# Recurrent-chunk keys transposed undecayed, the decay multiplied into the state's update

## The chip, the cores and the metric

One core of one Trainium2 chip runs the whole program. The metric is the device time of one execution in microseconds; the median of several runs is quoted, and lower is better. In the profile PE is TensorE (matmul), PEld its weight loads, DVE is VectorE, ACT is ScalarE, POOL is GpSimd and SP is SyncE, which issues the DMAs.

## The reference, cut to what matters

Two layers of a hybrid block are computed for 256 context and 256 latent tokens of width 2048: a modulated input projection, three groups of heads (retention, latent attention, RWKV-7) with gates, an output projection and a layer norm. The change lies in the RWKV-7 group, which scans the tokens in both directions:

```python
def step(state, inp):
    r_t, w_t, k_t, v_t, a_t, b_t = inp
    sa = jnp.einsum('dbhvk,dbhk->dbhv', state, a_t)
    state = state * w_t[..., None, :] + sa[..., :, None] * b_t[..., None, :] + v_t[..., :, None] * k_t[..., None, :]
    return state, jnp.einsum('dbhvk,dbhk->dbhv', state, r_t)
```

There are 8 heads of 64 channels. The kernel does this scan in chunks of 64 tokens, as matrix products.

## The kernel before, in words

**The work.** In each layer the 8 RWKV heads are done in two halves of 4 heads, and each half in two segments of 256 tokens (context, then latent): 4 segments a layer, 8 in all. A segment has 4 chunks, and both directions `d` are done side by side. The 4 heads of a half lie as 2 tiles `j` of 128 partitions, each with 2 heads `p` of 64 channels (partitions 0 to 63 and 64 to 127).

**A segment, in order.** `prepare` (L702 to L758) makes for each `(d, j)` the scaled queries `AR`, the scaled keys `bf` (channels on the partitions; b and k of each chunk side by side) and `pC`, the product of a chunk's decays for each channel. `grams` (L762) multiplies keys and queries (TensorE, L768), masks the result into `G` (VectorE, L772), and multiplies the keys by `pC` into `bs` (GpSimd, L776). `token_major` (L780) transposes `bs` on TensorE (L783) into a PSUM tile `bkT`, which ScalarE copies to `BK` (L784). `inverse_blocks` (L787) inverts 32x32 triangular blocks: transposes of `G` (L795), then a chain of 31 substitution steps on VectorE (L814, L817) in a tile `S` that GpSimd first fills (L801, L803), then transposes back (L822). `inverse_rest` (L826) completes the inverse with small matmuls `pA` and `pB` (L841), which need `TA` (L833).

**The scan** (L851) takes the 4 chunks in turn. For each: matmuls with the state (L905), with the inverse (L913), with the keys (L923, into the upper half of the PSUM tile `uz[d]`); then VectorE makes the new state `Zb` from that product and from `Zc` (L928 for the first chunk, L930 later), and GpSimd multiplies the new state by the next chunk's `pC` into `Zc` (`decayed`, L889). Then `values` (L866) transposes the next chunk's values on TensorE into the lower columns of the same PSUM tile `uz[d]` (L872, L874), VectorE copies them to `W` (L877), and `from_values` (L880) multiplies them (L884). Where the segment's outputs are wanted, the matmuls L937 stand between L923 and `values`; the context segments of the last layer have none. The last segment of a half needs no state after its last chunk: 28 updates of both directions in all, 24 of them followed by `values` in the same scan. During the scan, hooks call `prepare` for the next segment.

**Order.** TensorE's order is written by hand: `M(what)` lets a number of microseconds (table `FILL`, one set for each layer) of projection and adaptive-norm matmuls (L475, L431) run at that place, as filler under the latencies of the other engines. The order on VectorE, ScalarE and GpSimd is a scheduler's, which goes by priorities (`chain()` raises them) and by a simulated time; it also places the tiles, where tiles of one tag share slots. Tag `bs` has one slot, which `bs`, `S` and `Zc` take in turn. Tag `tb` has six, for `th`, `bf`, `Mt`, `TA` and others. Four PSUM slots (`sm`) hold `gram`, `bkT`, `uz`, `xy` and others.

Of the kernel before, what the change touches and what calls it, by code (L numbers as in the profile page):

```python
# [10 lines left out]
F32 = mybir.dt.float32  # L11
# [3 lines left out]
ALU = mybir.AluOpType  # L15
# [124 lines left out]
def hybrid_kernel(ctx, tc, I, out, dbg=None, layers=L):  # L140
    nc = tc.nc
    dma = nc.sync.dma_start
    act = nc.scalar.activation
    TT = nc.vector.tensor_tensor
    TS = nc.vector.tensor_scalar
    STT = nc.vector.scalar_tensor_tensor
    mm = nc.tensor.matmul

    def copy_a(o, i):
        act(out=o, in_=i, func=AF.Copy)  # L150
# [12 lines left out]
    def pbank(shape, name="sm"):  # L163
        return psm.tile(shape, F32, tag="sm", name=name)
# [5 lines left out]
    def K(name, n=128):  # L170
        o, e = CST[name]
        return cst[:n, o:e]

    idn = K("idn")
# [13 lines left out]
    with tc.tile_pool(name="ini", bufs=1) as ip:  # L188
# [9 lines left out]
        for l in range(layers):  # L198
            p, d = prT[l], dpr[l]
# [149 lines left out]
    def M(what):  # L349
        credit[0] += FILL[now[0]][what] if isinstance(what, str) else what  # L350
        while credit[0] > 0:
            t = next(mainline)
            if t == 0.0:
                settle(credit[0])
                credit[0] = 0.0
                return
            credit[0] -= t
            settle(t)
# [297 lines left out]
    def rwkv(rp, l, last):  # L656
        twl, al = state["lora", l]
        hs = lambda h: slice(64 * h, 64 * h + 64)
# [103 lines left out]
        def grams(S, d, j):  # L762
            ar, bf, mk, NY = S.AR[d], S.bf[d, j], masks[:, d], S.NY
            gps = [pbank([128, 4, 128], "gram") for p in range(2)]
            for i in range(4):
                for p in range(2):
                    hsl = slice(64 * p, 64 * p + 64)
                    mm(gps[p][:, i, :NY], lhsT=bf[hsl, i].rearrange("p a t -> p (a t)"),  # L768
                       rhs=ar[hsl, j, i, :NY], start=True, stop=True)
            for p in range(2):  # L770
                with chain():
                    TT(out=S.G[:, d, :, 2 * j + p, :NY], in0=gps[p][:, :, :NY],  # L772
                       in1=mk[:, :NY].unsqueeze(1).to_broadcast([128, 4, NY]), op=ALU.mult)

            bs = rp.tile([128, 4, 128], F32, tag="bs", name="bs", bufs=1)
            nc.gpsimd.tensor_tensor(out=bs, in0=bf.rearrange("p c a t -> p c (a t)"),  # L776
                                    in1=S.pC[d][:, j].unsqueeze(2).to_broadcast([128, 4, 128]), op=ALU.mult)
            return bs

        def token_major(S, d, j, bs):  # L780
            tp = pbank([128, 4, 128], "bkT")
            for i in range(4):
                nc.tensor.transpose(tp[:, i], bs[:, i], idn)  # L783
            act(out=S.BK[d][:, :, j, :], in_=tp, func=AF.Copy)  # L784

        def inverse_blocks(S):
# [66 lines left out]
        def scan(S, hook):  # L853

            rF, kF, vF = S.F
            s0, need, AR, BK, pC = S.s0, S.need, S.AR, S.BK, S.pC
            G = [S.G[:, d] for d in range(2)]
            Y = S.Y = rp.tile([128, 4, 256], F32, tag="Y", name="Y", bufs=1)
            Zc = rp.tile([128, 2, 2, 128], F32, tag="bs", name="Zc", bufs=1)
# [27 lines left out]
            def decayed(d, i):  # L887
                with chain():
                    nc.gpsimd.tensor_tensor(out=Zc[:, d], in0=Z[d],  # L889
                                            in1=pC[d][:, :, i:i + 1].to_broadcast([128, 2, 128]), op=ALU.mult)  # L890
# [9 lines left out]
            for i in range(4):  # L900
                for d in range(2):
                    if Z[d] is not None:
                        for j in range(2):
                            for r in halves:
                                mm(xy[d][r, 128 * j:128 * j + 128], lhsT=AR[d][:, j, i, r], rhs=Z[d][:, j, :],  # L905
                                   start=False, stop=(d == 1 and j == 1 and r.start == 0))
                with chain():
                    copy_a(Y[0:64, i % 2::2, :], xyt[0:64])
                hook(f"A{i}")
                M("xy")  # L910
                for d in range(2):
                    for h in range(4):
                        mm(uz[d][0:64, hs(h)], lhsT=G[d][0:64, i, h, 0:64], rhs=Y[0:64, 2 * d + i % 2, hs(h)],  # L913
                           start=True, stop=True)
                    with chain():
                        copy_a(W[d][0:64], uz[d][0:64, 0:256])
                M("u")
                if not (S.seg == 1 and i == 3):
                    for d in range(2):
                        zp = uz[d][:, 256:384].rearrange("p (j e) -> p j e", j=2)  # L920
                        for h in range(4):
                            j, p = divmod(h, 2)
                            mm(zp[hs(p), j], lhsT=BK[d][:, i, j, hs(p)], rhs=W[d][:, hs(h)], start=True, stop=True)  # L923
                        Zn = Zb[d][i % 2]
                        with chain():
                            for p in range(2):
                                if Z[d] is None:
                                    nc.vector.tensor_copy(out=Zn[hs(p), :, hs(p)], in_=zp[hs(p)])  # L928
                                else:
                                    TT(out=Zn[hs(p), :, hs(p)], in0=Zc[hs(p), d, :, hs(p)], in1=zp[hs(p)], op=ALU.add)  # L930
                        Z[d] = Zn
                        if i < 3:
                            decayed(d, i + 1)
                if need:
                    for d in range(2):
                        for h in range(4):
                            mm(xy[d][64:128, hs(h)], lhsT=G[d][0:64, i, h, 64:128], rhs=W[d][0:64, hs(h)], start=False,  # L937
                               stop=(d == 1 and h == 3))
                    for d in range(2):
                        c = 3 - i if d else i  # L940
                        if i < 2:
                            copy_a(Y[64:128, c], xy[d][64:128])
                        else:
                            TT(out=Y[64:128, c], in0=Y[64:128, c], in1=xy[d][64:128], op=ALU.add)
                if i < 3:
                    hook(f"B{i}")
                    M("zq")
                    for d in range(2):
                        values(d, i + 1)
                    M("zp")  # L950
                    for d in range(2):
                        from_values(d, i + 1)
# [47 lines left out]
        S, before = Segment(0), None  # L1000
# [3 lines left out]
        for n in range(4):  # L1004
# [8 lines left out]
            S.BK = [rp.tile([128, 4, 2, 128], F32, tag="BK", name="BK", bufs=2) for d in range(2)]  # L1013
            copies = []
            for d, j in ORDER:
                bs = grams(S, d, j)
                copies.append(lambda d=d, j=j, bs=bs: token_major(S, d, j, bs))
                M("gram")
                if len(copies) > 1:
                    copies.pop(0)()  # L1020
                M("tp")
# [23 lines left out]
            S = N  # L1045
# [589 lines left out]
```

## Time and profile before

| | |
|---|---|
| median of 3 runs | 2083.82 us (2076.26 to 2086.75) |
| the profiled execution's own time | 2067.83 us |
| its span, first to last instruction | 2066.1 us |
| PE busy | 1936.9 us, 94% |
| DVE busy | 1177.7 us, 57% |
| ACT busy | 768.8 us, 37% |
| POOL busy | 677.7 us, 33% |
| mean granted TensorE clock | 0.975 of full speed |

The RWKV segments lie at about 240 to 640 us (layer 0) and 1316 to 1730 us (layer 1) of the span. Busy time says little by itself: where PE is the busiest engine, what counts is where it stands idle, for how long, and at which clock it runs.

### The profile page before, as it was taken

To read this page: it belongs to the slowest core of one execution; us is meant where nothing else is said; L and a number is where in the kernel's file an instruction comes from. 1 tells how busy PE (TensorE), PEld (TensorE's weight loads), DVE (VectorE), ACT (ScalarE), POOL (GpSimd) and SP (SyncE) were. 2 spreads that over 40 slices of the span, in tenths; PEclk is the share of its full clock that TensorE was granted. 3 is DMA by queue.
4 is the path that set the end of the run, shared out by engine and by line. 5 is a ranking of instruction groups with operands and counts; after the bars stand their busy time and mean duration, and the time that the engine had idled before them with its cause. 6 is when DMAs were issued, how large, how long until landed. Compare 5 with 4: busy or idle time off the path is not lost. (4 is left out here: it accounts for less than half of the span.)

```text
span 2066.1 us, 35249 instructions
## 1 busy us (share of the span) xinstructions
PE 1936.9 (94%) x13222; PEld 1507.0 (73%) x13222; DVE 1177.7 (57%) x2905; ACT 768.8 (37%) x1443; POOL 677.7 (33%) x640
## 2 busy tenths in 40 slices
PE   6999999999999999999999989999799999899896
PEld 3567767676677687877788778776467678799875
DVE  3446576857662444445643582475648572564857
ACT  2223333333422444444222243332333334665542
POOL 0000444554534311223000175643335446323402
PEclk9999999999999999999999999997999999999998
DMA  9984453425255644449463343320822133534864
GB/s 327 368 266 118 120 157 107 151 80 169 62 169 188 197 147 138 134 131 334 136 194 128 108 138 107 89 83 18 310 82 78 41 107 113 171 108 130 268 230 163
DMA packets 255468, 318.42 MB, mean 154 GB/s; under 512 B 28288, under 2 KB 171968, under 8 KB 254400
## 3 DMA queue, kind: packets, MB, share of 16 engines
q1 hardware_dynamic: 255296, 316.16, 48.2%
q8 instruction: 104, 1.70, 0.3%
q14 instruction: 68, 0.56, 0.1%
HBM read 290.64 MB, written 25.46 MB: 153 GB/s over the span
## 5 line engine op out<-in xcount | busy, mean ns | idle before, releaser
L475 PE MATMUL pm<-H,whi 128*128 128x512 f32 (+2 forms) x2880 | 849.1, 375 | 12.8 <-DVE stg L634 4.1
L254 POOL TENSOR_TENSOR wlo<-raw,whi 128x512 fp32r<-128x512 f32 x332 | 438.9, 1329 | 989.5 <-ACT whi L253 885.8
L475 PEld LDWEIGHTS pm<-H,whi 128*128 128x128 f32 (+1 forms) x2880 | 513.9, 191 | 156.1 <-issue 55.6
L253 ACT ACTIVATE whi<-raw 128x512 fp32r<-128x512 f32 x556 | 348.9, 630 | 701.6 <-PE pm L475 356.7
L475 PE MATMUL pm<-H,wlo 128*128 128x512 f32 (+2 forms) x1440 | 536.1, 372 | 8.7 <-POOL wlo L254 8.7
L475 PEld LDWEIGHTS pm<-H,wlo 128*128 128x128 f32 (+1 forms) x1440 | 276.0, 192 | 62.0 <-issue 10.7
L254 DVE TENSOR_TENSOR wlo<-raw,whi 128x512 fp32r<-128x512 f32 x224 | 155.7, 700 | 187.0 <-ACT whi L253 172.7
L1411 PE MATMUL acc<-whi,Y 128*128 128x512 f32 x768 | 240.8, 393 | 0.5 <-ACT whi L253 0.5
L1411 PEld LDWEIGHTS acc<-whi,Y 128*128 128x128 f32 x768 | 143.5, 188 | 30.7 <-ACT whi L253 0.9
L1411 PE MATMUL acc<-wlo,Y 128*128 128x512 f32 x384 | 150.6, 392 | 0.2 <-DVE wlo L254 0.2
L814 DVE TENSOR_TENSOR stmp<-S,Mt 128x60 f32<-128x60 f32 (+14 forms) x488 | 110.9, 267 | 10.7 <-POOL S L803 10.6
L817 DVE TENSOR_TENSOR S<-S,stmp 128x60 f32<-128x60 f32 (+14 forms) x488 | 107.8, 261 | 0.4
L475 PE MATMUL pmx<-H,whi 128*128 128x512 f32 (+1 forms) x256 | 82.9, 402 | 14.7 <-ACT H L375 7.5
L431 PE MATMUL adap<-raw,scv 128*32 128x512 f32 x512 | 70.1, 620 | 15.1 <-DMA raw<-in_w_ada 11.8
L1411 PEld LDWEIGHTS acc<-wlo,Y 128*128 128x128 f32 x384 | 72.1, 188 | 15.8 <-DVE wlo L254 1.0
L150 ACT ACTIVATE Y<-xy 64x512 f32<-64x512 f32 (+1 forms) x56 | 26.7, 498 | 131.5 <-PE xy L905 99.3
L475 PEld LDWEIGHTS pmx<-H,whi 128*128 128x128 f32 x256 | 50.0, 206 | 31.6 <-DVE H L376 9.1
L751 DVE SCALAR_TENSOR_TENSOR bf<-th,kkF 128x256 f32<-128x256 f32 x32 | 16.3, 509 | 73.5 <-ACT th L726 73.2
L930 DVE TENSOR_TENSOR Zb<-Zc,uz 64x128 f32<-64x128 f32 x96 | 27.4, 285 | 52.7 <-PE uz L923 42.7
L889 POOL TENSOR_TENSOR Zc<-Zb,pC 128x256 f32<-128x256 f32 x56 | 33.9, 616 | 59.8 <-DVE Zb L930 31.0
L772 DVE TENSOR_TENSOR G<-gram,masks 128x512 f32<-128x512 f32 (+1 forms) x64 | 37.1, 620 | 23.5 <-PE gram L768 23.1
L475 PE MATMUL pmx<-H,wlo 128*128 128x512 f32 (+1 forms) x128 | 49.6, 388 | 0.0
(301 smaller groups left out, 2875.1 us busy)
## 6 DMA issues: line engine op xcount, KB each, us to landing
raw<-in_w_in SPq DMA_DIRECT2D x388, 256.0 KB, 3.0
raw<-in_w_ada SPq DMA_DIRECT2D x64, 1024.0 KB, 5.5
xraw<-in_w_ada SPq DMA_DIRECT2D x32, 1024.0 KB, 8.0
raw<-in_w_out SPq DMA_DIRECT2D x128, 256.0 KB, 3.9
raw<-in_mla_w_uq SPq DMA_DIRECT2D x48, 128.0 KB, 2.6
raw<-in_mla_w_ukv SPq DMA_DIRECT2D x32, 128.0 KB, 2.4
s_g<-stg SPq DMA_DIRECT2D x16, 256.0 KB, 4.2
gl<-s_g SPq DMA_DIRECT2D x16, 256.0 KB, 5.3
```

The source lines that it names most:

```text
L150: act(out=o, in_=i, func=AF.Copy)
L253: act(out=hi, in_=raw, func=AF.Copy)
L254: sub.tensor_tensor(out=lo, in0=raw, in1=hi.bitcast(F32), op=ALU.subtract)
L431: mm(st["ps"][32 * g:32 * g + 32, :], lhsT=sc(k + g), rhs=raw[:, g], start=(k == 0), stop=(k == KT - 4))
L475: mm(ps[p, i][:w], lhsT=x[:, o:o + w], rhs=H[y][:, a:], start=(k == k1 and n == 0), stop=(k == k2 - 1 and n == 2))
L751: STT(out=bf[:, :, 0], in0=ta, scalar=1.0, in1=kkv, op0=ALU.add, op1=ALU.mult)
L772: TT(out=S.G[:, d, :, 2 * j + p, :NY], in0=gps[p][:, :, :NY], in1=mk[:, :NY].unsqueeze(1).to_broadcast([128, 4, NY]), op=ALU.mult)
L814: TT(out=tv, in0=W32[:, r0:, s:s + 1].to_broadcast([128, n, b - a]), in1=Mt[s // 16][:, s % 16:s % 16 + 1, a:b].to_broadcast([128, n, b - ...
L817: TT(out=W32[:, r0:, a:b], in0=W32[:, r0:, a:b], in1=tv, op=ALU.add)
L889: nc.gpsimd.tensor_tensor(out=Zc[:, d], in0=Z[d], in1=pC[d][:, :, i:i + 1].to_broadcast([128, 2, 128]), op=ALU.mult)
L930: TT(out=Zn[hs(p), :, hs(p)], in0=Zc[hs(p), d, :, hs(p)], in1=zp[hs(p)], op=ALU.add)
L1411: mm(acc[cb, t], lhsT=Y[n][x][:, ts], rhs=y, start=(n == 0 and m == 0), stop=(n == KT - 1 and m == 2))
```

## The change

`grams` no longer makes `bs`; the keys `bf` themselves are transposed. The product of keys and values that comes out of L923 then lacks the factor `pC`, which belongs to its rows (the channels), and the update of the state multiplies it in, with `pC` as a scalar for each partition. That scalar differs between the two `j`, so one instruction per head takes the place of one for each `p`.

```diff
-            bs = rp.tile([128, 4, 128], F32, tag="bs", name="bs", bufs=1)
-            nc.gpsimd.tensor_tensor(out=bs, in0=bf.rearrange("p c a t -> p c (a t)"),
-                                    in1=S.pC[d][:, j].unsqueeze(2).to_broadcast([128, 4, 128]), op=ALU.mult)
-            return bs
-
-        def token_major(S, d, j, bs):
+        def token_major(S, d, j):
+
+            bf = S.bf[d, j]
             tp = pbank([128, 4, 128], "bkT")
             for i in range(4):
-                nc.tensor.transpose(tp[:, i], bs[:, i], idn)
+                nc.tensor.transpose(tp[:, i], bf[:, i].rearrange("p a t -> p (a t)"), idn)
             act(out=S.BK[d][:, :, j, :], in_=tp, func=AF.Copy)
...
-                            for p in range(2):
+                            for h in range(4):
+                                j, p = divmod(h, 2)
                                 if Z[d] is None:
-                                    nc.vector.tensor_copy(out=Zn[hs(p), :, hs(p)], in_=zp[hs(p)])
+                                    TS(out=Zn[hs(p), j, hs(p)], in0=zp[hs(p), j], scalar1=pC[d][hs(p), j, i:i + 1],
+                                       scalar2=None, op0=ALU.mult)
                                 else:
-                                    TT(out=Zn[hs(p), :, hs(p)], in0=Zc[hs(p), d, :, hs(p)], in1=zp[hs(p)], op=ALU.add)
+                                    STT(out=Zn[hs(p), j, hs(p)], in0=zp[hs(p), j], scalar=pC[d][hs(p), j, i:i + 1],
+                                        in1=Zc[hs(p), d, j, hs(p)], op0=ALU.mult, op1=ALU.add)
...
             for d, j in ORDER:
-                bs = grams(S, d, j)
-                copies.append(lambda d=d, j=j, bs=bs: token_major(S, d, j, bs))
+                grams(S, d, j)
+                copies.append(lambda d=d, j=j: token_major(S, d, j))
```

## Rows read from the trace of the kernel before

**Rows 1.** The page's busy line of PE: us, share of the span, instructions.

```profile
PE 1936.9 (94%) x13222; PEld 1507.0 (73%) x13222; DVE 1177.7 (57%) x2905; ACT 768.8 (37%) x1443; POOL 677.7 (33%) x640
```

**Rows 2.** PE's waits over the span: us in total, times, longest us.

```profile
PE bkT L783 <- POOL bs L776: 16.0, 11, 3.3
...
PE uz L872 <- DVE Zb L930: 4.2, 4, 2.5
...
PE uz L872 <- DVE Zb L928: 2.2, 4, 1.0
```

**Rows 3.** Timeline of the second segment's keys: start, us, instructions [idle before <-releaser].

```profile
369.51 1.04 POOL L776 TENSOR_TENSOR bs<-bf,pC 128x512 f32<-128x512 f32 x1
369.54 4.31 DVE L795 STREAM_TRANSPOSE Mt<-G 32x512 f32<-32x512 f32 x4
...
370.61 0.66 PE L783 MATMUL bkT<-cst,bs 128*128 128x128 f32 x4 [1.40 <-POOL bs L776]
...
374.94 1.12 PE L783 MATMUL bkT<-cst,bs 128*128 128x128 f32 x4 [2.52 <-POOL bs L776]
...
376.18 0.52 POOL L801 MEMSET S<- 128x512 f32 x1 [1.29 <-PE bkT L783]
...
377.08 0.26 DVE L814 TENSOR_TENSOR stmp<-S,Mt 128x16 f32<-128x16 f32 x2 [3.24 <-POOL S L803]
```

**Rows 4.** Timelines where the inverse is taken up, second and seventh segment.

```profile
406.71 1.29 DVE L833 STREAM_TRANSPOSE TA<-G 32x512 f32<-32x512 f32 x2
...
410.40 0.75 PE L841 MATMUL pA<-TA,G 32*32 32x32 f32 x64
...
1599.29 1.29 DVE L833 STREAM_TRANSPOSE TA<-G 32x512 f32<-32x512 f32 x2
...
1601.14 0.75 PE L841 MATMUL pA<-TA,G 32*32 32x32 f32 x64
```

**Rows 5.** DVE's groups by shape: busy us, mean ns of one | idle before.

```profile
L930 DVE TENSOR_TENSOR Zb<-Zc,uz 64x128 f32<-64x128 f32 x96 | 27.4, 285 | 52.7 <-PE uz L923 42.7 <-ACT whi L253 5.1 <-POOL rn L686 3.1
...
L944 DVE TENSOR_TENSOR Y<-Y,xy 64x256 f32<-64x256 f32 x24 | 9.2, 422 | 11.8 <-PE xy L937 11.7
...
L988 DVE SCALAR_TENSOR_TENSOR rkk<-yT,dpr,rkk 128x256 f32<-128x256 f32 x12 | 5.2, 478 | 0.1
...
L814 DVE TENSOR_TENSOR stmp<-S,Mt 128x16 f32<-128x16 f32 x16 | 2.9, 179 | 10.7 <-POOL S L803 10.6
```

**Rows 6.** Timelines of three state updates and the value transposes behind them.

```profile
423.01 1.20 DVE L930 TENSOR_TENSOR Zb<-Zc,uz 64x128 f32<-64x128 f32 x4 [2.87 <-PE uz L923]
...
425.92 0.60 PE L872 MATMUL uz<-cst,vF 128*128 128x128 f32 x4
...
1612.84 1.22 DVE L928 COPY Zb<-uz 64x128 f32<-64x128 f32 x4
...
1613.48 0.44 PE L872 MATMUL uz<-cst,vF 128*128 128x128 f32 x2 [0.84 <-DVE Zb L928]
...
1614.11 0.44 PE L872 MATMUL uz<-cst,vF 128*128 128x128 f32 x2 [0.18 <-DVE Zb L928]
...
1710.60 1.20 DVE L930 TENSOR_TENSOR Zb<-Zc,uz 64x128 f32<-64x128 f32 x4 [5.29 <-PE uz L923]
...
1712.04 0.60 PE L872 MATMUL uz<-cst,vF 128*128 128x128 f32 x4
```

**Rows 7.** Windows: from:to, us, busy time (instructions) of each engine, PEclk, DMA share, GB/s.

```profile
374.70:378.00 3.30, 3.06 (x14) 1.45 (x14) 0.90 (x5) 1.23 (x2) 1.48 (x5) 0.50 0.00 0
1566.00:1569.30 3.30, 3.30 (x9) 2.58 (x8) 1.18 (x6) 1.13 (x2) 2.55 (x5) 0.50 0.11 38
...
1412.40:1436.20 23.80, 23.12 (x110) 15.51 (x111) 10.26 (x27) 5.13 (x12) 6.10 (x11) 0.50 0.04 12
1611.00:1634.10 23.10, 20.22 (x174) 13.72 (x174) 13.82 (x35) 8.74 (x21) 12.96 (x18) 1.00 0.09 24
1634.20:1641.00 6.80, 6.80 (x33) 4.86 (x32) 4.76 (x9) 0.59 (x1) 3.04 (x5) 0.50 0.00 0
```

## The prediction, made before the changed kernel was run

> **What bounds the kernel now.** I read the busy line first: PE is busy 94% of the span [rows 1], so the time is PE's work, its idle time and the clock at which it works. The change takes nothing from PE's work: the transposes L783 have another source of the same shape, and no matmul is added. What can move is idle time and clock. So the second view is PE's waits [rows 2]: 16.0 us are spent in front of the key transposes, waiting for GpSimd's `bs`, and 6.4 us (4.2 + 2.2) in front of the value transposes, waiting for the state update `Zb`. The change ends the first and lengthens what the second waits for. The third view is the timeline at both places [rows 3, 6], and the last the granted clock behind the longer gaps [rows 7].
>
> **Removed: 32 multiplications on GpSimd.** In the second segment `bs` runs at 369.51 for 1.04 us and the transposes wait for it 1.40 us, then 2.52 us more for the next one [rows 3]. Read so, the eight segments lose 0.9, 3.9, 4.3, 2.6, 0.1, 0.9, 3.3 and 0.1 us, 16 in all. With `bf` as the source, which the grams before have already read, nothing here is late in its place: the PSUM banks of the grams are free by then (VectorE's next work, the transposes L795, begins at 369.54, before the first waiting transpose). I take the whole 16.0 us; the lower bound is in a rival.
>
> GpSimd also loses some 33 us of work (32 x 1.04), which I price at nothing: what PE waits for in these segments from GpSimd, besides `bs`, is a few microseconds of weight splits.
>
> **Moved: the filling of `S`.** The slot of tag `bs` is no longer held by keys. Before, the fill waited for the last key transposes (376.18, after 374.94), and VectorE stood idle 3.24 us before the substitution [rows 3]. It can now start when the transposes L795 end, at 369.54 + 4.31 = 373.85, 3.2 us earlier; the seventh segment gains as much. This matters, because PE comes earlier to the inverse too. In the second segment `TA` was ready at 408.00 and PE took it up at 410.40; in the seventh at 1600.58 and 1601.14 [rows 4]. Margins in all eight: 0.5, 2.4, 1.5, 1.8, 2.9, 27, 0.6 and 4.3 us. PE gains 3.9 us plus 1.7 of clock (next part) in the second against 2.4 + 3.2: a wait of 0.1 us. In the seventh it gains 3.3 + 1.7 against 0.6 + 3.1: a wait of 1.3. With 0.3 in the first and 0.1 in the third, 1.8 us of the gain are given back.
>
> **The clock behind these gaps.** After the gaps of the second segment the granted clock is 0.50 (1.2 instead of 2.4 GHz) from 374.7 to 378, and the same transposes take 1.12 instead of 0.66 us [rows 3, 7]; after the seventh's it is 0.50 from 1566.0 to 1569.3. Work at half speed costs at most half of such a stretch, 1.7 us each: 3.4 us gained where the gaps go.
>
> **Added: eight short updates in place of four.** A chunk's update is now 8 instructions of 64x64 with a scalar per partition, where it was 4 of 64x128. No row shows that form, so I build the price: 285 ns for 64x128, less 64 columns at (422 - 285)/128 = 1.07 ns, is 217 ns; an instruction with a scalar per partition costs 478 against 422 ns at 256 columns, 56 ns more [rows 5]. Together 273 ns. Halving the columns buys nothing. Four updates take 1.20 to 1.22 us [rows 6], 15 to 20 ns more than their durations each, so I take 0.287 us as the pace and 2.3 us for all eight. The first direction's state is then 0.55 us later, the second's 1.1 us.
>
> What waits is `values`: it writes into the PSUM tile from which the update reads. Behind it on PE stand `from_values` and the whole next chunk, so what it loses the program loses. Three kinds of step are seen [rows 6]:
> - At 1612.84 PE already waits, 0.84 and 0.18 us. The whole 1.1 us is added. Six of the 24 steps are such, all in the last layer, five of them in its context segments, which have no L937 matmuls as cover: 6.8 us.
> - At 1710.60 PE goes on at 1712.04, with the second direction's transposes at 1712.25; the new end is 1710.60 + 2.3 and some 0.09 of hand-over, 1712.99. That is 0.74 us. Nine steps lose 0.3 to 1.0 us so: 5.7 us.
> - At 423.01 the new end is 425.4, and PE comes at 425.92. Nine steps lose nothing; the matmuls L937, the hooks' and the filler hide it. With that cover gone each would lose 1.1 us.
>
> In all 12.4 us, 3.5 of them in layer 0. The ends: without the 56 ns for the scalar the same count gives 6.1 us; at 0.30 us an update, 14.1. Four updates are followed by the next segment's grams instead, which need the slots of `uz`: I allow 0.6 us. The copies to `W` and the outputs' additions queue behind the longer update on VectorE; whoever needs them stands on PE behind the value transposes, which wait for the same update, so I add nothing for them.
>
> A pair of L814 takes 0.26 us at 0.179 each [rows 3, 5]: there the second starts about 0.1 us before the first ends, while the updates, which alternate between the two partition halves, do not overlap [rows 6]. The Trainium skill, "VectorE: DVE Perf Modes", section "Two Vector instructions with no wait between them", has this as a rule: an instruction whose operands start in another quadrant than the one before is held until all earlier ones have finished. The new order still alternates, so by that rule all eight are held and the sum stands at 12.4; without it the price is that of the second rival.
>
> **The clock in the last layer's scans.** From 1412.4 to 1436.2 the clock is 0.50, after a wait of 2.5 us for `Zb`, the longest in that row [rows 2, 7]. In the other context segment of that layer it holds at 1.00 through waits of 0.8 to 1.0 us until 1634.1 and is then 0.50 for 6.8 us. The change makes these waits 1.1 us longer: 2 us, between what was borne and what was not. If the clock fell at the first of them, some 10 us more of the first scan and 20 us of the second would run at half, at most 15 us of loss (an estimate, half of those stretches). I take a bit over a quarter, 4 us. The Trainium skill, "TensorE: Matmul & The Clock Gate", section "HAM oscillation — how this bites in real kernels", says that pauses of the matmul stream, not only long stages, cost the clock; the gaps above agree.
>
> **Sum.** -16.0 - 3.4 + 1.8 + 12.4 + 0.6 + 4.0 = -0.6 us on the profiled execution's 2067.83. That execution is 16 us under the median of the runs shown, 2083.82; I carry the difference over to the median: 2083 us. A measurement of this kernel tells about 0.5%, 10.4 us, from no change.
>
> **Rivals.**
> - *The clock falls in both context scans of the last layer* (slower). For it: the 24 us at half clock after one wait of 2.5 us. Against: the other scan bore three waits of about 1 us. Full price 15 us in place of 4: -16.0 - 3.4 + 1.8 + 12.4 + 0.6 + 15 = +10.4, 2094 us. It decides once some 30 us more of those scans run at half.
> - *The short updates overlap, or most of their length is hidden* (faster). Each would start about 0.1 us before the last one ends, as L814 does, at a pace under 0.19 us: 2 us in place of 12.4, and hardly a reason for the clock to fall. -16.0 - 3.4 + 1.8 + 2 + 0.6 = -15, 2069 us. Against it: four L930 need 1.2 us.
> - *Another wait takes the place of `bs`*: the mask of the grams on VectorE, which holds the PSUM slots and is queued behind the norm and the longer update, or the inverse. Then perhaps 4 of the 19.4 us come in: -4 + 12.4 + 0.6 + 4 = +13, 2097 us. Against it: at 369.54 VectorE is past the masks.
> - *The scheduler's order on VectorE, ScalarE and GpSimd shifts elsewhere*, since its simulated time changes: either sign, some microseconds.
>
> **How the numbers follow.** The trade as summed 0.50, the clock 0.17, overlap 0.18, another wait 0.10, a shifted order 0.05. The trade has its own range of 2074 to 2092: the price of the updates from 6.1 to 14.1, and the runs' spread of 5 us to either side. The whole range is 2066 to 2098; it takes in the rivals' times with part of that spread. Faster by over 0.5%, below 2073.4: most of the overlap case and a little of the trade and the order, 0.17. Slower, above 2094.2: half of the clock case, most of the other wait, a little of the rest, 0.19. Within: 0.64.
>
> **What would show it.** Right: no wait of `bkT` for anything on GpSimd; `S` filled before the last key transposes; eight updates of about 0.27 us that take 2.3 us from first to last; some 19 us of waits of the value transposes for `Zb` in place of 6.4, mostly in the last layer; PE's busy time unchanged but for the clock. Wrong: updates that overlap, key transposes that still wait a microsecond or more, `pA` waiting for `TA` by several microseconds, or a long stretch of 0.50 at 1611 to 1634.

## The result, and the profile of the changed kernel

The changed kernel takes 2111.26 us in the median of 4 runs (2100.13 to 2115.55), the kernel before 2085.28 on the same chip (2076.26 to 2089.22): a ratio of 1.0142, interval 1.011 to 1.0173. It is slower by 1.4%, where the forecast was no difference, and the time lies 13 us above the range. The profiled execution took 2110.16 us; that of before, 2067.83, lies low among the times of its kernel, so the two profiles stand 42 us apart and the medians 26.

TensorE runs the same 13222 matmuls in the same order. The page's busy line, then PE's waits [rows 1, 2]:

```profile
PE 1971.9 (94%) x13222; PEld 1531.9 (73%) x13222; DVE 1215.8 (58%) x3017; ACT 769.3 (36%) x1443; POOL 643.3 (31%) x608
```

```profile
PE uz L869 <- DVE Zb L929: 10.4, 14, 3.1
...
PE uz L869 <- DVE Zb L926: 6.2, 6, 1.7
PE pA L838 <- DVE TA L830: 6.2, 5, 4.0
```

No wait of the key transposes is left. The waits for the state update grew from 6.4 to 16.6 us, and a new one, `pA` for `TA`, has 6.2. But PE's busy time grew by 35 us, with no matmul added: that is the clock.

The keys of the second segment, where two gaps stood [rows 3]:

```profile
374.91 0.60 PE L780 MATMUL bkT<-cst,bf 128*128 128x128 f32 x4
375.34 4.45 DVE L792 STREAM_TRANSPOSE Mt<-G 32x512 f32<-32x512 f32 x4
376.51 0.60 PE L780 MATMUL bkT<-cst,bf 128*128 128x128 f32 x4
379.82 1.19 DVE L811 TENSOR_TENSOR stmp<-S,Mt 128x16 f32<-128x16 f32 x2
```

No bracket stands behind the transposes: nothing was waited for. VectorE goes from the transposes L792 straight into the substitution, without the 3.24 us idle of before.

Where PE takes up the inverse, second and seventh segment [rows 4]:

```profile
409.41 0.66 DVE L830 STREAM_TRANSPOSE TA<-G 32x512 f32<-32x512 f32 x1
410.47 0.75 PE L838 MATMUL pA<-TA,G 32*32 32x32 f32 x64
...
1619.88 1.29 DVE L830 STREAM_TRANSPOSE TA<-G 32x512 f32<-32x512 f32 x2
1620.73 0.32 PE L838 MATMUL pA<-TA,G 32*32 32x32 f32 x4 [3.95 <-DVE TA L830]
1621.32 1.06 PE L838 MATMUL pA<-TA,G 32*32 32x32 f32 x60 [0.28 <-DVE TA L830]
```

In the second segment PE still comes 0.4 us after `TA`. In the seventh it stands still 4.2 us, and behind that the 64 small matmuls take 1.38 us instead of 0.75.

The updates by shape [rows 5], and one in the last layer with the value transposes behind it [rows 6]:

```profile
L929 DVE SCALAR_TENSOR_TENSOR Zb<-uz,pC,Zc 64x64 f32<-64x64 f32 x192 | 54.4, 283 | 61.0 <-PE uz L920 48.0 <-ACT whi L253 9.1 <-POOL bf L758 0.5
...
L926 DVE TENSOR_SCALAR Zb<-uz,pC 64x64 f32<-64x64 f32 x32 | 9.1, 284 | 0.6
```

```profile
1636.33 2.39 DVE L926 TENSOR_SCALAR Zb<-uz,pC 64x64 f32<-64x64 f32 x8
1637.57 0.44 PE L869 MATMUL uz<-cst,vF 128*128 128x128 f32 x2 [1.51 <-DVE Zb L926]
1638.77 0.44 PE L869 MATMUL uz<-cst,vF 128*128 128x128 f32 x2 [0.77 <-DVE Zb L926]
```

Last the clock [rows 7]. Windows over the scans of the fifth to seventh segment, a stretch of the last of them, and two neighbouring stretches in layer 0:

```profile
1400.90:1450.30 49.40, 43.11 (x292) 28.24 (x291) 24.76 (x63) 12.85 (x31) 14.47 (x23) 0.76 0.07 23
1526.00:1572.10 46.10, 44.78 (x493) 34.83 (x490) 26.41 (x69) 15.66 (x38) 16.57 (x28) 0.89 0.08 22
1625.80:1679.70 53.90, 50.87 (x293) 35.30 (x289) 25.28 (x63) 14.94 (x34) 17.01 (x23) 0.62 0.06 16
...
1639.40:1677.00 37.60, 36.85 (x179) 25.82 (x178) 17.97 (x42) 9.44 (x21) 11.67 (x17) 0.50 0.06 15
...
413.30:420.90 7.60, 7.60 (x85) 5.43 (x86) 1.79 (x5) 1.35 (x4) 2.29 (x3) 1.00 0.98 332
420.90:431.10 10.20, 10.20 (x74) 8.47 (x74) 3.41 (x10) 2.04 (x5) 3.55 (x3) 0.50 0.13 44
```

Right behind the update of the timeline above, at 1639.4, the clock goes to 1.2 GHz and stays there for 37.6 us. In the kernel before that stage was at 0.50 for 6.8 us.

The two profiles by stages (from the first gram to the last key transposes; from there to the end of `pB`; the scans; the rest), each with its length, PE's idle time and the time at half clock (granted 0.50, 1.2 GHz), in us, added up from the traces:

| | keys | inverse | scans | rest | all |
|---|---|---|---|---|---|
| before: length | 113.6 | 324.5 | 351.7 | 1276.3 | 2066.1 |
| idle / half clock | 16.5 / 1 | 22.3 / 19 | 11.2 / 31 | 79.2 / 53 | 129.2 / 104 |
| after: length | 97.0 | 339.9 | 392.4 | 1279.0 | 2108.4 |
| idle / half clock | 2.2 / 0 | 31.7 / 39 | 21.0 / 94 | 81.7 / 66 | 136.5 / 199 |

The keys gained 16.6 us. The inverse gave back 15.4. The scans lost 40.7, with only 9.8 us more of idle time.

### The profile page after: what moved, and what is told of

Its sections match the earlier page's. It is cut to its first block, busy times and chain, and to the rows that moved or that the text cites. A ratio compares the mean times of both kernels' runs of the same rounds, so it can differ in the third digit from the quotient of the medians.

```text
span 2108.4 us, 35287 instructions
## 1 busy us (share of the span) xinstructions
PE 1971.9 (94%) x13222; PEld 1531.9 (73%) x13222; DVE 1215.8 (58%) x3017; ACT 769.3 (36%) x1443; POOL 643.3 (31%) x608
## 5 line engine op out<-in xcount | busy, mean ns | idle before, releaser
L475 PE MATMUL pm<-H,whi 128*128 128x512 f32 (+2 forms) x2880 | 860.1, 379 | 14.4 <-DVE stmp L811 4.7
L475 PEld LDWEIGHTS pm<-H,whi 128*128 128x128 f32 (+1 forms) x2880 | 521.1, 194 | 161.7 <-issue 58.8
L475 PE MATMUL pm<-H,wlo 128*128 128x512 f32 (+2 forms) x1440 | 540.4, 375 | 10.1 <-POOL wlo L254 10.1
L929 DVE SCALAR_TENSOR_TENSOR Zb<-uz,pC,Zc 64x64 f32<-64x64 f32 x192 | 54.4, 283 | 61.0 <-PE uz L920 48.0
L150 ACT ACTIVATE Y<-xy 64x512 f32<-64x512 f32 (+1 forms) x56 | 26.7, 498 | 154.1 <-PE xy L902 118.0
L751 DVE SCALAR_TENSOR_TENSOR bf<-th,kkF 128x256 f32<-128x256 f32 x32 | 15.4, 480 | 80.3 <-ACT th L726 80.0
L414 PE MATMUL adap<-xraw,scv 128*32 128x512 f32 (+1 forms) x320 | 37.2, 566 | 13.8 <-DVE lg L233 10.8
```

The source lines that it names most:

```text
L414: mm(ps[32 * g:32 * g + 32, :cn], lhsT=sc(kc + q), rhs=raw[:, q], start=(kc + q < 4), stop=(kc + q >= KT - 4))
L475: mm(ps[p, i][:w], lhsT=x[:, o:o + w], rhs=H[y][:, a:], start=(k == k1 and n == 0), stop=(k == k2 - 1 and n == 2))
L929: STT(out=Zn[hs(p), j, hs(p)], in0=zp[hs(p), j], scalar=pC[d][hs(p), j, i:i + 1], in1=Zc[hs(p), d, j, hs(p)], op0=ALU.mult, op1=ALU.add)
```

## The experiments

Theory after this: the longer updates make PE pause in the scans, the clock falls behind such pauses, and that costs more than the pauses; the gain at the keys is given back at the inverse. Rivals: the clock falls with the thin matmuls of a scan (products of 64-channel heads) whether PE pauses or not, or by chance; or the undecayed keys do harm by themselves. All ratios below are to the kernel before, run on the same chip.

**The two halves of the change.** The first run takes the keys alone: undecayed keys, and the four long updates as before, with a constant in place of the decay.

```diff
-                            for h in range(4):
-                                j, p = divmod(h, 2)
+                            for p in range(2):
...
-                                    STT(out=Zn[hs(p), j, hs(p)], in0=zp[hs(p), j], scalar=pC[d][hs(p), j, i:i + 1],
-                                        in1=Zc[hs(p), d, j, hs(p)], op0=ALU.mult, op1=ALU.add)
+                                    STT(out=Zn[hs(p), :, hs(p)], in0=zp[hs(p)], scalar=1e-17,
+                                        in1=Zc[hs(p), d, :, hs(p)], op0=ALU.mult, op1=ALU.add)
```

> The keys' half of the change alone: undecayed keys are transposed, and the state's update keeps its four instructions of 64x128, with a constant of 1e-17 in place of the chunk's decay (the decay itself is left out, so the output is not the reference's). Theory (the longer update costs, the removal gains): no wait of the key transposes, some 16 us less idle in the key stages than before, waits of the value transposes as before (some 7 us), time 2062 to 2074. Rival (the removal itself costs, by segments that lie closer together, by the order that the scheduler makes, or by the clock): 2085 or more.

2078.96 us, ratio 0.9986 (0.9953 to 1.0019): neither. The waits for `bs` are gone, those for `Zb` stay at 6.8 us, and no time comes out of it. `pA` waits for `TA` 6.1 us.

The second run takes the updates alone: `bs` stays, and the updates are eight with a scalar that is one.

```diff
+            one = K("rst")[:, 0:1]
...
-                                    TT(out=Zn[hs(p), :, hs(p)], in0=Zc[hs(p), d, :, hs(p)], in1=zp[hs(p)], op=ALU.add)
+                                    STT(out=Zn[hs(p), j, hs(p)], in0=zp[hs(p), j], scalar=one[hs(p), 0:1],
+                                        in1=Zc[hs(p), d, j, hs(p)], op0=ALU.mult, op1=ALU.add)
```

> The update's half alone: bs is still made with the decay, as before the change, and the state's update is done by eight instructions of 64x64 with a scalar for each partition, which is a one. Theory: updates of 2.4 us, value transposes waiting 14 to 20 us in place of 6.6, more of the scans at half clock, key transposes waiting 16 us as before, time 2105 to 2130. Rival (the removal costs): 2085 to 2095.

2122.18 us, ratio 1.0198 (1.0138 to 1.0258). Eight updates take 2.39 us, the waits for `Zb` are 12.4 us, and the mean clock of its runs is 0.9515, against 0.967 of before. The waits are under the 14 to 20 expected, the time is in the theory's range. The updates alone make more than the whole loss.

**The same updates in another order**, both `j` of one partition half and then the other half; on all engines the rest keeps its order:

```diff
-                                j, p = divmod(h, 2)
+                                p, j = divmod(h, 2)
```

> The changed kernel with the eight updates in another order: both j of one partition half in turn, so that within a pair the next instruction works on the same partitions. If changing the partition half is what keeps an update from starting before the last one has ended: 1.9 to 2.0 us for eight in place of 2.38, waits of the value transposes down by 4 to 6 us, time 2095 to 2107. If it is something else: 2.38 us and 2106 to 2115.

2089.48 us, ratio 1.0048 (1.0017 to 1.0078), 1% better than the change from the order alone, and under the 2095 to 2107 expected. The timeline has the update:

```profile
1414.61 1.99 DVE L929 SCALAR_TENSOR_TENSOR Zb<-uz,pC,Zc 64x64 f32<-64x64 f32 x8
```

0.40 us less each, and the waits for `Zb` are 10.5 us instead of 16.6. Six microseconds of waits stand against some 20 us of time; the mean clock is 0.9605.

**More filler under the update** (it is taken from other places):

```diff
-    dict(zq=0.7, end0=17.28, a0=3.38, a1=0.7, ada=2.41, begin=3.59, sq=2.6, nr=8.0, z0=5.0,
+    dict(zq=1.8, end0=17.28, a0=3.38, a1=0.7, ada=2.41, begin=3.59, sq=2.6, nr=8.0, z0=5.0,
...
-    dict(zq=0.2, end0=15.71, ada=6.79, begin=9.04, sq=1.32, nr=8.31, z0=5.0, gram=0.5, tp=0.3,
+    dict(zq=1.3, end0=15.71, ada=6.79, begin=9.04, sq=1.32, nr=8.31, z0=5.0, gram=0.5, tp=0.3,
```

> The changed kernel with 1.1 us more of projection matmuls between the state's update and the value transposes (zq 1.8 and 1.3). Theory: the waits of the value transposes fall from 16.6 to under 5 us, and the scans at half clock to 60 us or less; the filler is missing later, which costs little: 2080 to 2095. Rival (the clock falls in the scans because their matmuls are thin, waits or not, or the filler is missed as much where it was taken): 2100 to 2112.

2091.32 us, ratio 1.0038 (1.0008 to 1.0069). The time is in the theory's range. The waits for `Zb` fell to 6.7 us (under 5 expected), but the next matmuls now wait for the copies to `W`, which stand behind the update on VectorE:

```profile
PE xy L881 <- DVE W L874: 10.4, 10, 2.5
PE uz L869 <- DVE Zb L926: 5.2, 6, 1.9
...
PE uz L869 <- DVE Zb L929: 1.5, 3, 0.8
```

**The decay on GpSimd.** The update is a plain addition of the product to the old state, four instructions again, and GpSimd multiplies the sum by the chunk's `pC`; `Zc` is no longer needed.

```diff
-                    nc.gpsimd.tensor_tensor(out=Zc[:, d], in0=Z[d],
+                    nc.gpsimd.tensor_tensor(out=Zb[d][1], in0=Zb[d][0],
                                             in1=pC[d][:, :, i:i + 1].to_broadcast([128, 2, 128]), op=ALU.mult)
...
+                            for p in range(2):
+                                if Z[d] is None:
+                                    nc.vector.tensor_copy(out=U[hs(p), :, hs(p)], in_=zp[hs(p)])
+                                else:
+                                    TT(out=U[hs(p), :, hs(p)], in0=Z[d][hs(p), :, hs(p)], in1=zp[hs(p)], op=ALU.add)
+                        decayed(d, i)
```

> The keys are transposed undecayed as in the change, but the decay is multiplied into the state by GpSimd after a plain addition on VectorE (state = pC x (old state + product)), so that the update is four instructions of 64x128 again and no addition to Zc is left. It computes the same as both. Theory (the longer update cost the time through the waits it made and the clock behind them, and the keys' own gain is nearly all given back at the inverse): updates of 1.2 us as before, waits of the value transposes 6 to 7 us, mean clock 0.963 to 0.968, pA waits for TA of 4 to 8 us, and a time of 2066 to 2086, no more than 0.7% under before. Rival 1 (GpSimd now stands on the way of the state): the state products L899 wait for Zb from GpSimd, 5 us or more in all, and the time is 2088 or more. Rival 2 (undecayed keys cost something by themselves): 2090 or more with no such wait.

2079.96 us, ratio 0.9988 (0.9957 to 1.002), as the theory has it: no wait for GpSimd's state, 5.7 us for `Zb`, 4.2 for `TA`. The mean clock, 0.9614, is a little under the 0.963 to 0.968 expected. With the filler at the inverse raised as well (`inv2` from 15 to 17 and from 17 to 20):

> The kernel of the run before, with more filler matmuls between the key transposes and pA (inv2 from 15 to 17 us in layer 0, from 17 to 20 in layer 1; they are taken from the places between the stages). Theory (the gain at the keys was given back because PE now comes to pA before TA is ready): the waits of pA for TA fall from 4 to 8 us to 2 or less, and the time is 5 to 12 us under that of the run before. Rival (the waits of pA were no loss of their own, the same time is lost wherever PE gets ahead of the other engines): the waits turn up at the first matmuls after the scans, and the time is within 4 us of the run before.

2075.62 us, ratio 0.9978 (0.9942 to 1.0015). A miss for the theory: `pA` waits 8.2 us, because in the last segment the substitution took 35 us instead of the 24 of the changed kernel and PE waited 7.9 us there; elsewhere the waits are gone. The time changed by no more than can be told.

**The values in a PSUM tile of their own**, so that they need not wait for the update that reads `uz`:

```diff
+                vt = uz[d] if need else xy[d]
...
-                        nc.tensor.transpose(uz[d][:, 128 * j:128 * j + 128], flat[:, a - 64:a + 64], idn)
+                        nc.tensor.transpose(vt[:, 128 * j:128 * j + 128], flat[:, a - 64:a + 64], idn)
```

> The change as it is, but in the two segments without outputs (context segments of the last layer) the values are transposed into the PSUM tile of xy, whose upper half is free there, so that they no longer wait for the update that reads uz. The updates stay as they are, 2.4 us for eight. Theory (it is PE's waiting at these places that takes the clock): the value transposes' waits for Zb fall from 16.6 to 6 or 7 us, some 2 to 5 us of waits of L903 for Zb appear instead, the stretch at half clock in the context scan of the last half falls from 41 to under 20 us, and the time from 2111 to 2085 to 2100. Rival (the clock there falls because of the thin matmuls alone, waits or not): the stretch stays over 30 us and the time stays at 2100 to 2112.

2112.88 us, ratio 1.0147 (1.0092 to 1.0203), and 62 us at half clock in the last context scan. The pause was not taken away, only renamed; it ends with the copies to `W`, queued behind the same updates:

```profile
PE xy L870 <- DVE W L875: 8.6, 6, 3.0
...
PE uz L870 <- DVE Zb L930: 4.3, 8, 0.8
```

PE is idle in the scans for 19.5 us, as good as the 21.0 of the changed kernel, and the clock is as bad. It can't tell the theories apart. The same holds for the run that joins it with the other order and the filler:

> The change with the run before's PSUM tile for the values, the update's eight instructions in the other order (both j of one partition half, then the other half; 2.0 us instead of 2.4) and the filler at the inverse (inv2 17 and 20). It computes the same. Theory: waits of the value transposes for Zb of 4 to 6 us, waits of pA for TA of 2 us or less, mean clock 0.965 or more, and a time of 2055 to 2078, under before. Rival (the clock falls by chance in the scans, whatever the waits): clock 0.955 to 0.962 and a time of 2080 or more.

2105.15 us, ratio 1.0095 (1.0062 to 1.0128), mean clock 0.9554: the waits for `Zb` and `TA` are as the theory has them (4.5 and 0.9 us), but its clock and its time failed, and the rival's hold. It does not decide for the rival, because the pauses were not taken away: the `W` waits are 10.1 us, PE is idle in the scans for 20.0, and the order's gain is lost again.

**Both kernels once more**, for a second profile of each:

> The kernel before, unchanged, for a second profile (the first was one of its fastest runs). Theory (a part of the fall of the clock is chance, and the last layer's scans are where it is most often lost): a time of 2070 to 2092; the key transposes wait for bs as before (15 to 17 us) and the value transposes for Zb 6 to 7 us; time at half clock 100 to 170 us, in other stretches than in the first profile, but under 50 us of it inside the scans. Rival (each kernel loses the clock in fixed places): the same stretches as in the first profile.

> The changed kernel, unchanged, for a second profile. Theory: a time of 2098 to 2118; the same waits within 10%; 170 to 230 us at half clock, 75 us or more of it inside the scans, the long stretch in the context scan of the last half (41 us in the first profile) or of the half before it there again. Rival (the first profile's stretches were chance): under 60 us at half clock inside the scans.

2071.39 and 2120.81 us, the second a little over the expected times. Before again has 32 us at half clock in the scans (31 in the first profile), 24 of them in one stretch in the fifth segment as in the first; the changed kernel has 119 (94), with 42 (41) in the seventh. So the loss in the scans is not chance. The waits did not repeat within 10%: those for `Zb` are 12.2 us instead of 16.6, and PE is idle in the scans for 16.8 us instead of 21.0, with more time at half clock than in the first profile. How much the clock loses is thus not set by the length of the pauses alone. The rival falls for the changed kernel; for the kernel before, the theory was wrong in that its one long stretch lies in the same place in both profiles. The windows of the same three scans as above, before and then after:

```profile
1395.10:1441.60 46.50, 42.83 (x291) 28.10 (x291) 21.91 (x51) 12.85 (x31) 14.42 (x23) 0.74 0.08 24
1514.60:1554.40 39.80, 39.69 (x492) 31.24 (x488) 22.91 (x57) 15.62 (x37) 16.16 (x25) 1.00 0.08 21
1607.20:1643.50 36.30, 33.41 (x291) 23.37 (x291) 20.33 (x51) 14.53 (x34) 18.09 (x23) 1.00 0.10 29
```

```profile
1400.10:1453.00 52.90, 49.46 (x291) 32.15 (x291) 24.74 (x63) 13.14 (x31) 14.55 (x23) 0.61 0.07 21
1529.40:1580.80 51.40, 50.58 (x490) 39.05 (x490) 26.62 (x69) 15.69 (x37) 18.62 (x30) 0.77 0.07 20
1637.70:1692.00 54.30, 51.27 (x289) 35.70 (x289) 24.40 (x62) 14.93 (x34) 17.50 (x23) 0.61 0.06 16
```

**Covering the pauses with work that nobody needs.** Ahead of the value transposes of the second and third chunk, in the two segments without outputs:

```diff
+                    if not need and i < 2:
+                        cover = pbank([128, 256], "cover")
+                        for n in range(14):
+                            mm(cover, lhsT=masks[:, 0], rhs=masks.rearrange("p d t -> p (d t)"), start=True, stop=True)
                     for d in range(2):
                         values(d, i + 1)
```

> The changed kernel with 14 matmuls of 128x256 (bf16, into a PSUM tile of their own that nobody reads) in front of the value transposes of the second and third chunk in the two segments without outputs: four places, where PE waits 1 to 4 us for the update. Nothing is left out, it is work added, at most 6 us of it at the full clock. Theory (the pauses take the clock in these scans): the value transposes' waits fall by 5 us or more, the time at half clock in these two scans falls from 65 us to under 30, and the time to 2090 to 2102. Rival (in these scans the clock falls with the thin matmuls, pauses or not): it stays at 50 us or more in them and the time at 2105 to 2116.

2108.64 us (2087.73 to 2113.38), ratio 1.0123 (1.0059 to 1.0187): undecided. The time is in the rival's range, and the 40 us at half clock that stay in the two scans lie between the two. 6.8 us of work were added. But the cover was too short, as the timeline shows; where it ends PE still pauses, and at 1427.5 the clock falls:

```profile
1423.12 1.70 PE L951 MATMUL cover<-masks 128*128 128x256 bf16 x14
1426.36 0.44 PE L869 MATMUL uz<-cst,vF 128*128 128x128 f32 x2 [1.54 <-DVE Zb L929]
1427.57 0.69 PE L869 MATMUL uz<-cst,vF 128*128 128x128 f32 x2 [0.77 <-DVE Zb L929]
```

So the same with 30 matmuls:

> The changed kernel with 30 matmuls in place of 14 at the same four places, so that they last longer than the update (some 3.3 us at the full clock). It computes the same. With 14 of them PE still paused 1.5 and 0.8 us there. Theory (pauses take the clock): no wait of more than 0.3 us at these places, under 20 us at half clock in the two scans (40 with 14, 65 without), at the price of some 5 us more of added work: 2090 to 2104. Rival (it is the thin matmuls): 40 us or more at half clock in them and 2108 or more.

2086.49 us (2079.05 to 2093.56), ratio 1.0017 (0.9985 to 1.005), under the theory's range even. 13.8 us of useless matmuls make the changed kernel 25 us faster (by the ratios, 1.0142 and 1.0017, 1.2%). Timeline and the windows of the two covered scans:

```profile
1418.40 3.45 PE L951 MATMUL cover<-masks 128*128 128x256 bf16 x30
1421.68 0.39 PE L869 MATMUL uz<-cst,vF 128*128 128x128 f32 x2
1422.84 0.44 PE L869 MATMUL uz<-cst,vF 128*128 128x128 f32 x2 [0.77 <-DVE Zb L929]
```

```profile
1398.90:1439.40 40.50, 38.77 (x349) 27.30 (x349) 25.33 (x62) 12.71 (x31) 14.39 (x23) 1.00 0.09 28
...
1613.40:1659.70 46.30, 44.27 (x353) 32.92 (x351) 24.75 (x63) 14.61 (x34) 17.48 (x23) 0.86 0.06 18
```

The first scan is 8.9 us shorter than in the changed kernel, though it has half of the added work, and its clock is 1.00 throughout; the second has 13 us at half instead of 41. The thin matmuls are the same ones. (A wait of 0.77 us for the second direction's update stayed, more than the 0.3 expected, and did no harm in the first.)

The short cover on the version with GpSimd's decay and filler, on the kernel before, and on GpSimd's decay without that filler:

> The kernel with the decay on GpSimd and more filler at the inverse, with the same 14 matmuls at the same four places. It computes the same as both. Theory: the 24 and 14 us at half clock in the two scans fall under 20 together, and the time is 2064 to 2074, under before by 0.3 to 0.8%. Rival (added matmuls cost what they take): 2076 to 2084.

> The kernel before, with the same 14 matmuls at the same four places and nothing else. It computes the same. Theory (the pauses in front of the value transposes take the clock in the scan of the last layer's third segment from the end, also before the change): the 24 us at half clock there go, PE's wait of 2.5 us for Zb too, and the time is 2066 to 2076, 2 to 8 us under before; the rest of the 15 us that the version with GpSimd's decay, filler and cover has over before belongs to the undecayed keys. Rival (the undecayed keys are worth nothing, the cover is all): 2058 to 2066.

> The decay on GpSimd with the cover, without the added filler at the inverse. It computes the same. Theory (the filler at the inverse was worth 4 us at most): 2060 to 2070, clock 0.970 or more, waits of pA for TA of 4 us. Rival (the filler is what made the difference, by the clock in the stages behind it): 2072 to 2080.

2061.83 us (ratio 0.9926, 0.9897 to 0.9955), 2069.35 (0.9937, 0.9912 to 0.9962) and 2069.14 (0.9931, 0.9901 to 0.9961). All three beat both kernels, and they can't be told from each other by their intervals. In the profile of the first of them the two covered scans are at 1.00:

```profile
1389.30:1424.80 35.50, 35.48 (x328) 24.91 (x328) 21.26 (x51) 14.78 (x34) 16.97 (x24) 1.00 0.12 30
...
1595.60:1632.40 36.80, 35.69 (x317) 25.95 (x317) 20.73 (x51) 14.07 (x33) 17.32 (x24) 1.00 0.08 23
```

The expectation set out from 24 and 14 us at half clock in these scans. In the profile of this version without the cover it is 0 and 13.7 us, so the cover took away some 14 us there.

The kernel before with only the cover gains as much as the others: the stretch of 24 us at half clock in its fifth segment is gone. Its time is in the theory's range, but the undecayed keys add nothing that these runs can tell, which is what its rival said of them.

The cover did not hold the clock each time. The windows of the first covered scan, in the kernel before with the cover and in GpSimd's decay with the cover alone:

```profile
1394.10:1430.50 36.40, 35.30 (x318) 24.14 (x318) 20.75 (x51) 12.72 (x31) 15.03 (x23) 1.00 0.10 30
```

```profile
1391.20:1436.70 45.50, 44.40 (x319) 29.68 (x319) 21.90 (x51) 12.81 (x31) 14.43 (x23) 0.77 0.09 24
```

Behind the second cover, ahead of the third chunk's values, PE pauses for 0.92 and 0.18 us in both. In the first the clock stays full; in the second it is at half from 1414.0 on, for 20.5 us. That execution, 2076.58 us, was the longest of its kernel.

## Why the prediction was wrong

**A scale for the clock.** Each run comes with its time and its mean granted clock. (1 - mean clock) x 2 x time is its time at half clock. A fit over 193 runs of all these kernels, with one constant for each kernel and one common slope, gives 0.37 us of time for each microsecond at half clock, and leaves 2.4 us unexplained. The first profiles of the two kernels give the same (35.0 us more of busy PE for 95 us at half), the second profiles 0.50 (47.9 for 96). So the fit splits each difference in two as an estimate:

| kernel | mean clock | us at half clock | to before, at equal clock | PE idle in the scans |
|---|---|---|---|---|
| before | 0.967 | 137 | 0 | 11.2 |
| changed | 0.951 | 206 | +5.4 | 21.0 |
| keys alone | 0.964 | 149 | -8.2 | 11.0 |
| updates alone | 0.9515 | 206 | +16.9 | 18.9 |
| other order | 0.9605 | 165 | 0.0 | 15.1 |
| GpSimd's decay | 0.961 | 161 | -9.2 | 9.2 |
| changed, 30 cover | 0.970 | 124 | +11.3 | 14.9 |
| before, 14 cover | 0.9745 | 106 | +0.9 | 6.5 |

The clock and the times are means over the runs of a kernel (5 of the changed one, with the second profile); the idle time is that of its profile.

**The sum by stages.** Keys and inverse together came to -1.2 us (-2.7 in the second profiles) where the sum had -16.0 - 3.4 + 1.8 = -17.6, and the scans to +40.7 (+45.9) where it had 12.4 + 0.6 + 4.0 = 17.0. So two things failed: what the keys gain was nearly all given back, and the clock's fall in the scans was priced far too low. The second is the larger.

**The wait for `bs`** (-16.0): right, nothing is left of it, and the keys are 16.6 us shorter in the first profiles (10.7 in the second, where the changed kernel ran 13 us of them at half clock). Of the 3.4 us of clock behind these gaps nothing remained: keys and inverse together have 39 us at half clock, against 20 before (38 against 33 in the second profiles).

**Given back at the inverse** (+1.8): mis-sized. PE is idle there 9.4 us longer (22.3 to 31.7). The waits before the key transposes stood where VectorE was still at work on the inverse, and they had hidden that work. I let the substitution start 3.2 us earlier. Counted from the segment's first gram, `TA` was ready 2.9 us earlier in the second segment (46.6 instead of 49.5), but only 0.3 us in the seventh (49.1 instead of 49.4), where the substitution itself took 29.4 us instead of 26.7 and PE then waited 4.2 us instead of 1.3. In the first and the fourth segment it was even 1.1 and 0.5 us later. In the second profile the waits for `TA` are 4.2 us in all, the longest 1.9; so a part of this varies between executions. `pA` and `pB` ran at half clock for 10 us (0.5 before) and took 28.9 us over the eight segments instead of 23.9. In the second profiles it is the other way round (4 us in the changed kernel, 10 in the one before), so this is not shown to come from the new pauses. Keys alone are worth 8 us at equal clock where -16.0 + 1.8 would make 14; in time the runs can't tell them from nothing, and they have 12 us more at half clock.

**The updates** (+12.4): right in the mechanism and nearly in size. 283 ns an instruction (priced 273), 2.39 us for eight (2.3), 16.6 us of waits for `Zb` (19; 12.2 in the second profile). At equal clock the updates alone cost 16.9 us. The pace bears out the rule that I named, of the Trainium skill, "VectorE: DVE Perf Modes", section "Two Vector instructions with no wait between them": an instruction that starts in another quadrant than the one before is held. The other order, in which the second of each pair, four of eight, starts where the last one did, took 1.99 us for the same eight instructions, some 0.1 us less for each of the four: the trace agrees, and the overlap rival falls with it for the order that was used.

**The clock in the last layer's scans** (+4.0): this is the step that failed. Of the 31 us between the means, some 26 are clock by the fit (69 us more at half, times 0.37); with the 3.4 us that I credited to it my net was 0.6. My rival, that the clock falls in both context scans of the last layer, had the mechanism, but capped at 15 us in two scans. It fell in all four scans of that layer (in three of them in the second profile) and in the second segment's in layer 0. In the fifth segment, where the kernel before had already lost 24 us, the first profile has no more than that; the second has 41. I had argued from the pauses of about 1 us that one scan of before bore without a fall; with pauses of 1.5 and 0.8 us in that same scan the changed kernel went to half clock for 37.6 us. That the longer updates are the cause is shown by the updates alone, which have the same 69 us more at half clock. That they act through the pauses is shown in the main: the other order shortens the pauses, adds no work and has 41 us less at half in the mean of its 10 runs, and with the long cover the same thin matmuls run at 1.00 in the first scan and have 13 us at half instead of 41 in the second. One rival is left: the covers also add matmuls of 128x256, which may keep the clock up by themselves, and no run fills a pause without such matmuls. Against it stands that 14 of them in each place did not hold the clock where pauses of 1.5 and 0.8 us remained.

The Trainium skill, "TensorE: Matmul & The Clock Gate", section "HAM oscillation — how this bites in real kernels", counts half of the throttled time as lost. The runs agree in kind; the fit gives 0.37, and the second pair of profiles by itself comes to the half. By one half the 69 us would be an estimated 35 us, more than the 31 that were lost.

**The scheduler's order** did shift: apart from the updates and `bs`, 27 of VectorE's 2793 instructions, 17 of ScalarE's 1443 and 28 of GpSimd's 592 stand elsewhere in their engine's order. No run shows what this cost. The rival of a wait in the place of `bs` is true of the inverse, but not of the mask that I named.

What stays open: with the keys alone and with GpSimd's decay PE is idle in the scans no longer than before, and yet there are 12 to 24 us more at half clock. In both profiles of the changed kernel the clock also falls in the second segment's scan in layer 0, as the window from 420.9 shows, after 7.6 us in which PE had no pause at all; in neither of before it does. The profiles of the keys alone and of GpSimd's decay have it too (6.8 and 10.2 us). And behind a pause of the same length the clock fell in one profile and not in another, as the two windows with the short cover show. Pauses explain the bulk, and not this.

## What to carry to other kernels

Price a wait of TensorE in a stage of thin matmuls by what it does to the clock, not by its length: here 10 us more of pauses in the scans came with 69 us more at half clock, which by the fit cost some 26 us where all the rest of the change cost 5. Where such a pause can't be taken away, try to fill it to its end: under the longer updates the short cover left pauses of 1.5 and 0.8 us and 40 us at half clock, and the long one, 13.8 us of matmuls that nobody reads, paid for itself. A wait that is removed ahead of an inverse or any other long chain is worth only what the chain behind it can follow.

## What the runs showed of the hardware

- 13.8 us of matmuls that nobody reads made a kernel 25 us faster (2111.26 to 2086.49), and 6.8 us of them made the kernel before 12 us faster (2081.35 to 2069.35).
- A small VectorE instruction took as long as the GpSimd instruction that started with it. An addition of 128x16 to `S` took 1.29 us beside GpSimd's split of a weight, where another on 128x16 took 0.18; this held the substitution up in the seventh segment:

```profile
1613.95 1.29 POOL L254 TENSOR_TENSOR wlo<-raw,whi 128x512 fp32r<-128x512 f32 x1 [1.43 <-ACT whi L253]
1613.99 1.29 DVE L814 TENSOR_TENSOR S<-S,stmp 128x16 f32<-128x16 f32 x1
```

- Eight updates of the same shape took 2.39 or 1.99 us, by nothing but the order of their partition halves.
